# Smaller weight units, four buffers instead of two, and a page table loaded earlier

## The chip, the cores and the metric

The kernel runs on one core of a Trainium2 chip. The metric is the device time of one execution in microseconds (us). A core has a matrix engine (TensorE, PE in the rows, with its weight loads as PEld), a vector engine (VectorE, DVE), a scalar engine (ScalarE, ACT), a general engine (GpSimd, POOL), and a sync engine (SyncE, SP) that here only issues DMAs. Sixteen DMA engines move data between the main memory and the on-chip buffer.

## The reference, cut to what matters

A prompt of 256 tokens and eight samples of one token each go through two layers that share one set of weights; they are handled as one matrix of NT = 264 columns and 1024 features.

```
layer 0: x += 0.5*SwiGLU(rms(x)); x += W_out[gated delta net | differential attention](W_in rms(x)); x += 0.5*SwiGLU(rms(x))
layer 1: x += 0.5*SwiGLU(rms(x)); x += latent attention(rms(x));                                     x += 0.5*SwiGLU(rms(x))
y = rms(x)
swiglu(h) = (silu(h @ w_gate) * (h @ w_up)) @ w_down        # w_gate, w_up: 1024 x 2816, w_down: 2816 x 1024
past keys and values of a sample = pool[page_table[sample]]  # 16 pages of 128 rows
```

So there are four feed-forward parts (FFN 0 to 3), one mixer between 0 and 1 and one between 2 and 3. The samples attend to 2048 past rows each, which lie in pages that the page table names.

## The kernel before, in words

**Weights.** The host lays all weight matrices out as 2600 blocks of 128 x 128 float32 numbers in the order of their use. The class `Stream` (object `W`) brings them in units of 16 blocks (1 MB, 128 rows of 8 KB) into two buffers of the pool tag `raw` (`N_RAW = 2`, line 33). A piece is 4 blocks. `split` (line 618) turns a piece into a high part, written by ScalarE, and a low part, written by VectorE, in one of six places `whl`; three matrix products per block then give float32 accuracy. Splitting runs up to `LOOK = 5` pieces ahead of the blocks that PE uses. When the last piece of a unit is split, `used` (line 613) makes the next load into that buffer, by a DMA on the SP queue. A few weights of the second mixer are used whole, without a split (`whole`, line 650). `W.limit` holds the splitting back in each mixer, because its attention borrows the `whl` places, and `W.resume` lets it go on.

**Stages.** The first FFN is fed by `boot` (line 1082), which scales x by the norm weights and takes its squares. An FFN (line 864) computes 22 pairs of gate and up columns and then 8 down columns, block after block. The mixer of layer 0 (line 1143) interleaves the input projection `proj`, the prompt's and the samples' differential attention and the delta net. The mixer of layer 1 (line 1781) does the same for latent attention, and ends in `tail` (line 2057), the output projection.

**Past rows.** Two `Loader` objects gather strips of pages by indirect DMAs that GpSimd issues. `LK` gathers keys (tiles `dk`, 512 KB each, 64 of them, and later `mk`), `LV` gathers values (`dv`, 1 MB each, 32 of them, and later `mv`). They need the row numbers in `pt` and `ptk`, which `early` (line 1095) computes on VectorE from the page table. The first gathers are made in FFN 0: after column m, `side[m]()` hands a free place to a loader.

**The order of work.** The program is written as threads (generators). The class `Clock` (line 188) replays them with a cost estimate for every instruction and puts each instruction into its engine's queue in the order of the estimated starts, once, while the program is built; on the chip every queue runs in that fixed order. A DMA is estimated at 450 ns of the hardware queue, 700 ns of delay, its bytes at 360 GB/s on one pipe that all DMAs share, and 1000 ns (lines 460 to 467). Where the estimate leaves PE a gap, `keep_warm` (line 436) puts products of a constant into it that nobody reads (line 666). A thread can wait for a name (`yield from wait(...)`) that another thread makes available with `done.add`; a `flow` thread otherwise goes on as soon as few of its products are left to put into the queue.

**The start.** SP issues, in this order: the norm vectors, x in three parts with the first unit in three parts between and behind them, the second unit, the identity matrix, the page table, the constants, and the rest (lines 703 to 731).

Of the kernel before, what the change touches and what calls it, by code (L numbers as in the profile page):

```python
# [32 lines left out]
N_RAW = 2  # L33
# [87 lines left out]
N_UNITS = (N_BLOCKS + 15) // 16  # L121
# [21 lines left out]
class Virtual:  # L143
    """A tile whose place is chosen when its first instruction is put into a queue."""
# [5 lines left out]
class Slots:  # L150
    """Places of one shape for virtual tiles. The place of a tile is free again when its thread has gone past the
    segment that made it (keep: when the thread has called free) and its last instruction is in a queue."""
# [35 lines left out]
class Clock:  # L188
    """Puts the instructions that the threads create into the engine queues in the order of their
    estimated starts, so that no queue waits long at its head."""  # L190
# [16 lines left out]
    # -- tiles  # L207
# [48 lines left out]
    def when(self, r, write, eng=None):  # L256
        """When an instruction of `eng` may use the region."""
        n, p0, p1, lo, hi = r
        l = self.reg.get(n)
        if l is None and n[0] == "v" and n[1:].isdigit() and self.virtual[int(n[1:])].at is None:  # L260
            return self.virtual[int(n[1:])].slots.first(eng)[0]
        if l is None and self.prev.get(n):
            l, (p0, p1, lo, hi), write = self.reg.get(self.prev[n], ()), (0, 128, 0, 1 << 30), True
        t = 0.0
        for a in l or ():
            if a[0] < p1 and p0 < a[1] and a[2] < hi and lo < a[3]:
                if a[4]:
                    t = max(t, a[4] + self.lag(a[6], eng))
                if write and a[5]:
                    t = max(t, a[5] + self.lag(a[7], eng))  # L270
        return t
# [18 lines left out]
    # -- cost estimates  # L290
# [47 lines left out]
    # -- instructions  # L338
# [91 lines left out]
    def pe(self, t, c, cols, share):  # L430
        """The tensor engine's clock is halved in each tick after one in which few columns left the array."""
        if self.columns.get(int(t // self.TICK) - 1, 0.0) < self.FULL:
            c *= 2.0
        k = int((t + c) // self.TICK)
        self.columns[k] = self.columns.get(k, 0.0) + cols * share
        return t + c

    def keep_warm(self, t):
        """Matmuls that nobody reads, up to time t."""
# [52 lines left out]
    def add(self, name):  # L492
        """What the current thread has created so far makes `name` available."""
        if not self.cur:
            self.done[name] = 0.0
        else:
            self.cur.marks.append((name, self.seq))
            self.settle(self.cur)

    # -- threads: generators that yield None (go on when all that they issued is done), a time, or the  # L500
    # names they wait for
# [53 lines left out]
def hybrid_trunk_kernel(ctx: ExitStack, tc: tile.TileContext, wall, xT, wba, vecs, cst0, cst1, ident_d, convst,  # L555
# [29 lines left out]
    def service(thread, f, *a):  # L585
        """f's instructions in a thread of their own, which nobody waits for as a whole."""
# [5 lines left out]
    # ------------------------------------------------------------ weight stream  # L592
    class Stream:
        """The weights, 128 x 128 blocks in the order of their use; units of 16 blocks are loaded, pieces of 4 split into
        a high and a low part, except those that raw() hands out whole."""
# [7 lines left out]
        def dma(self, *parts):  # L603
            if self.u < N_UNITS:
                if self.u not in self.raw:
                    self.raw[self.u] = wp.tile([128, 2048], F32, tag="raw", name="raw", bufs=N_RAW)
                    self.left[self.u] = 16 // PIECE
                for a, b in parts or ((0, 2048),):
                    Q.dma_start(self.raw[self.u][:, a:b], wall[self.u][:, a:b])
                if not parts or parts[-1][1] == 2048:  # L610
                    self.u += 1
# [6 lines left out]
        def split(self):  # L618
# [4 lines left out]
            u, o = divmod(p * PIECE, 16)  # L623
# [11 lines left out]
        def advance(self, p):  # L635
            while self.p <= p + LOOK and self.p < self.limit and self.p * PIECE // 16 < self.u:
                self.split()
# [12 lines left out]
        def whole(self, use):  # L650
            """use(the next block); with float32 products for these there is nothing to split."""
            p, s = divmod(self.i, PIECE)
            u, o = divmod(self.i, 16)
# [11 lines left out]
    # in the tensor engine's gaps it multiplies a constant, so that its clock stays up  # L665
# [17 lines left out]
    def rsqrt(src, w, np_=128):  # L683
        """1/sqrt of a small tile on the vector engine."""
# [17 lines left out]
    # ------------------------------------------------------------ constants  # L702
# [8 lines left out]
    W.dma((1024, 2048))  # L711
    for _ in range(N_RAW - 1):
        W.dma()
# [10 lines left out]
    Q.dma_start(pt, ptab)  # L724
    cst = sb.tile([128, NCST], F32, tag="cst", name="cst0")
# [7 lines left out]
    # ------------------------------------------------------------ norm statistics  # L733
# [19 lines left out]
    def norm_rows(n, squares, scale, eps):  # L753
        """squares: n tiles [128, NT]. For tile i, rows 32 i and 32 i + 1 of the result add up to
        1 / sqrt(scale * (sum over the partitions) + eps)."""
# [32 lines left out]
    class Rstd:  # L788
        """The thread that computes mul / sqrt(scale * sum of acc over the partitions + eps), for every row; get()
        yields it to a thread that needs it."""  # L790
# [31 lines left out]
    # ------------------------------------------------------------ driver  # L822
# [7 lines left out]
    def flow(gen, bonus=0.0):  # L830
        """A thread that goes on as soon as its matrix products are in the queue."""
        return gen, True, bonus

    def urgent(gen, bonus=BONUS):
        """A thread whose instructions go first even if others could start a little earlier."""
# [8 lines left out]
    def lead(xh, xl, tags):  # L844
        """The first blocks of a projection; the last rows of x come latest, so the first two blocks alternate."""
# [17 lines left out]
    # ------------------------------------------------------------ FFN  # L863
    def ffn(f, wname, woff, rs, last=False, side={}):
        xh, xl = state["xw"]
        with tc.tile_pool(name=f"ffn{f}", bufs=1) as ap_:
# [21 lines left out]
            for m in range(MF):  # L888
# [14 lines left out]
                if m in side:  # L903
                    side[m]()
# [17 lines left out]
    # ------------------------------------------------------------ final norm  # L922
# [18 lines left out]
    def finish_y():  # L941
        """The statistics with the tokens on the partitions; a product with their diagonal spreads them."""
# [21 lines left out]
    # ------------------------------------------------------------ KV gather  # L964
# [5 lines left out]
    class Loader:  # L970
        """Gathers tiles of 32-row strips of four pages each, in order, into whichever slots are free."""
# [40 lines left out]
        def retire(self, tags):  # L1012
            """These slots are not filled again."""
# [8 lines left out]
    # ------------------------------------------------------------ one sample's softmax over its past  # L1022
    def scores(b, w, load, parts, SM, ready, cc, P, pT):
        """w [128, sub, 32]: the queries, one diagonal block for each page of a strip; parts: for each part
        of the features, its four strips' tiles. Leaves exponentials (strip, page, query row; key) in P,
        transposed in pT; returns the inverses of their sums."""
# [30 lines left out]
    def weigh(o, pT, load, strips, vs, dv):  # L1057
        """o [32 j + query row, dv]: the values weighed by pT."""
# [13 lines left out]
    # ============================================================ start  # L1072
# [22 lines left out]
    def early():  # L1095
        V.tensor_scalar(pt, pt, 32.0, vc("pi"), op0=OP.mult, op1=OP.add)
        for i in range(2):
            V.tensor_scalar(ptk[:, i, :], pt[:, 0:4 * NS], 2.0, float(i), op0=OP.mult, op1=OP.add)
        yield
# [42 lines left out]
    # ============================================================ layer 0 mixer  # L1142
    def mixer0():
        with tc.tile_pool(name="m0", bufs=1) as mp_:
# [16 lines left out]
            # ---- input projection  # L1161
# [70 lines left out]
            # ---- normalisation of four head blocks by their partition sums  # L1232
# [13 lines left out]
            # ---- gated delta net  # L1246
# [19 lines left out]
            def gdn():  # L1266
# [59 lines left out]
                # decay in (key, query) layout, 64-token chunks stacked two high  # L1326
# [12 lines left out]
                # Gram products  # L1339
# [60 lines left out]
                # token-major keys and values  # L1400
# [24 lines left out]
                # scan over the chunks  # L1425
# [29 lines left out]
            # ---- gated delta net, one step of each sample: four samples at a time, row 32 j + 4 i + h  # L1455
            # belongs to sample 4 t + j and head h (i: high, low and again high part of the update's operands)
# [110 lines left out]
            # ---- differential attention, prompt  # L1567
# [90 lines left out]
            # ---- differential attention, samples  # L1658
# [46 lines left out]
            # ---- output projection, one half of the rows at a time  # L1705
# [24 lines left out]
            def post_d():  # L1730
# [10 lines left out]
                # the samples: rows (head, sample), columns the head's features  # L1741
# [38 lines left out]
    # ============================================================ layer 1 mixer  # L1780
    def mixer1():
        with tc.tile_pool(name="m1", bufs=1) as mp_:
# [139 lines left out]
            # ---- prompt  # L1922
# [44 lines left out]
            # ---- samples  # L1967
# [43 lines left out]
            def mla_self():  # L2011
                yield from wait("ql0", "ql1", "qp", "ck")
                # scores of the new tokens with themselves: rows h, columns b
# [71 lines left out]
# ---- host side: layouts only  # L2085
def _blocks(w):
    """[K, M] -> [M/128, K/128, 128, 128] (m block, k block, row, column)."""
# [4 lines left out]
def _pack(inp):  # L2092
# [4 lines left out]
    def pairs(a):  # L2097
        """Blocks of two columns at a time, their first halves first."""
# [35 lines left out]
    if n % 16:  # L2134
        a = np.concatenate([a, np.zeros((16 - n % 16, 128, 128), f)], 0)
    return np.ascontiguousarray(a.reshape(N_UNITS, 16, 128, 128).transpose(0, 2, 1, 3)).reshape(N_UNITS, 128, 2048)

# [76 lines left out]
```

## Time and profile before

| | us |
|---|---|
| median of 3 runs | 1344.3 |
| range of the runs | 1342.52 to 1350.92 |
| span of the profiled execution, first to last instruction | 1297.2 |

The profiled execution's own device time is not listed apart from its span. The median of the runs lies 47.1 us above the span, which is time before the first and after the last instruction.

In the profile, busy time is given by engine, and idle time by what ended it. Rows of a view by windows give, for each stretch, the busy time of each engine with its count of instructions, the granted TensorE clock as a share of full speed (1.00 is 2.4 GHz, half of it is 1.2 GHz), the share of the 16 DMA engines' time that packets took, and the rate in GB/s. The chain of waits is followed back from the last instruction. Nearly all instructions go through one helper (line 457), so rows are told apart by the tiles that they write and read.

### The profile page before, as it was taken

The numbers are of one execution on the slowest core, as the hardware profiler recorded it, in microseconds if no ns is written. First come the engines' busy times: TensorE is split into PE (matmuls) and PEld (weight loads), VectorE is DVE, ScalarE is ACT, GpSimd is POOL, SyncE is SP. The second block draws the span as 40 slices with busy tenths as digits, with TensorE's granted clock in tenths as the row PEclk, the third lists the DMA queues.
The fourth block names the chain that finished last, engine by engine and source line by source line (L and its number), as shares of the span: only waits on it lengthen the run. The fifth ranks groups of instructions, "written<-read, shape, count | busy, mean of one in ns | idle before, by whom it ended". The sixth has DMA issues, their size and how long they took to land.

```text
span 1297.2 us, 28444 instructions
## 1 busy us (share of the span) xinstructions
PE 1274.9 (98%) x11569; PEld 1146.7 (88%) x11569; DVE 874.0 (67%) x1855; ACT 580.7 (45%) x1185; POOL 433.4 (33%) x526
## 2 busy tenths in 40 slices
PE   9999999999999999999999999999999999999997
PEld 7999999967676567999999999999876679999996
DVE  6777667687762767877766777766874449777652
ACT  5555544345411024555554555544432235555541
POOL 3643222355552412553422222212334523322221
PEclk9999999999996879999999999999999999999999
DMA  7776556898897563676755454555467955555551
GB/s 286 264 272 233 192 168 229 285 342 320 304 344 288 167 229 133 230 282 221 260 167 192 163 194 168 191 171 187 161 240 278 393 166 176 191 181 178 195 167 63
DMA packets 52163, 287.72 MB, mean 222 GB/s; under 512 B 6192, under 2 KB 6768, under 8 KB 27200
## 3 DMA queue, kind: packets, MB, share of 16 engines
q1 hardware_dynamic: 28912, 180.77, 40.0%
q0 software_dynamic: 23120, 105.13, 22.3%
q8 instruction: 91, 1.49, 0.4%
q14 instruction: 40, 0.33, 0.1%
HBM read 280.95 MB, written 5.03 MB: 220 GB/s over the span
## 4 chain that ended last, share of the span: by engine, by line
PE 86%; DVE 5%; DMA 3%; issue 2%; ACT 1%; POOL 1%; SPq 0%; POOLq 0%; ACTq 0%; DVEq 0%
PE ps_pd L457 40%; PE ps_pa L457 37%; PE ps_pc L457 5%; PE ps_po L457 3%; DVE whl L457 2%; PE ps_pe L666 2%; DMA dv<-in_vpool_dram,pt 2%; DMA raw<-in_wall_dram 1%; ACT whl L457 0%; DVE wxl L457 0%; DMA x<-in_xT_dram 0%; DVE QW L457 0%; DVE x L457 0%; POOL t L457 0%; DVE QR L457 0%
## 5 line engine op out<-in xcount | busy, mean ns | idle before, releaser
L457 DVE TENSOR_TENSOR whl<-raw,whl 128x512 fp32r<-128x512 f32 x642 | 486.0, 766 | 214.7 <-ACT whl L457 208.3
L457 ACT ACTIVATE whl<-raw 128x512 fp32r<-128x512 f32 x642 | 399.8, 630 | 371.9 <-PE ps_pa L457 195.9
L457 PE MATMUL ps_pa<-wxh,whl 128*128 128x264 f32 x1616 | 325.0, 286 | 1.8 <-ACT t L457 0.8
L457 PEld LDWEIGHTS ps_pa<-wxh,whl 128*128 128x128 f32 x1616 | 260.8, 188 | 11.0 <-issue 6.6
L457 PE MATMUL ps_pd<-wxh,whl 128*128 128x264 f32 x1152 | 233.9, 285 | 0.0
L457 PE MATMUL ps_pa<-wxl,whl 128*128 128x264 f32 x808 | 231.1, 286 | 0.0
L457 PEld LDWEIGHTS ps_pd<-wxh,whl 128*128 128x128 f32 x1152 | 187.6, 188 | 0.9 <-DVE whl L457 0.4
L457 POOL TENSOR_TENSOR t<-t,t 128x264 f32<-128x264 f32 (+1 forms) x100 | 83.1, 831 | 275.6 <-DVE t L457 275.4
L457 PE MATMUL ps_pd<-wxl,whl 128*128 128x264 f32 x576 | 164.1, 285 | 0.0
L457 PEld LDWEIGHTS ps_pa<-wxl,whl 128*128 128x128 f32 x808 | 151.8, 188 | 4.9 <-issue 4.5
L457 PE MATMUL ps_pd<-ah,whl 128*128 128x264 f32 x704 | 130.9, 284 | 0.0
L457 PE MATMUL ps_pa<-ah,whl 128*128 128x264 f32 x704 | 130.7, 284 | 0.0
L457 PEld LDWEIGHTS ps_pd<-ah,whl 128*128 128x128 f32 x704 | 110.0, 188 | 0.0
L457 PEld LDWEIGHTS ps_pa<-ah,whl 128*128 128x128 f32 x704 | 109.9, 188 | 0.0
L457 PEld LDWEIGHTS ps_pd<-wxl,whl 128*128 128x128 f32 x576 | 108.2, 188 | 0.8 <-issue 0.8
L457 PE MATMUL ps_pd<-al,whl 128*128 128x264 f32 x352 | 99.9, 284 | 0.0
L457 PE MATMUL ps_pa<-al,whl 128*128 128x264 f32 x352 | 99.7, 283 | 0.0
L457 POOL TENSOR_TENSOR al<-t,ah 128x264 fp32r<-128x264 f32 x88 | 76.9, 874 | 58.0 <-ACT ah L457 57.9
L457 POOL TENSOR_TENSOR t<-x 128x264 f32<-128x264 f32 x45 | 32.8, 730 | 189.0 <-DVE x L457 183.3
L457 POOL DMA_INDIRECT dk<-in_kpool_dram,ptk x57 | 58.8, 1031 | 56.9 <-PE ps_pc L457 45.2
L457 PE MATMUL ps_pd<-wya,whl 128*128 128x264 f32 x352 | 71.2, 284 | 0.0
L457 PE MATMUL ps_pa<-wya,whl 128*128 128x264 f32 x352 | 71.0, 284 | 0.0
(414 smaller groups left out, 1964.6 us busy)
## 6 DMA issues: line engine op xcount, KB each, us to landing
raw<-in_wall_dram SPq DMA_DIRECT2D x162, 1024.0 KB, 4.9
out_y_dram<-wya SPq DMA_DIRECT2D x4, 264.0 KB, 2.6
xh<-in_rec_dram SPq DMA_DIRECT2D x4, 256.0 KB, 9.5
xl<-in_rec_dram SPq DMA_DIRECT2D x4, 256.0 KB, 17.6
out_recs_dram<-xh SPq DMA_DIRECT2D x4, 256.0 KB, 7.1
out_recs_dram<-xl SPq DMA_DIRECT2D x4, 256.0 KB, 4.3
dk<-in_kpool_dram,ptk POOLq DMA_INDIRECT x57, 6.3
cst<-in_cst_dram SPq DMA_DIRECT2D x1, 838.5 KB, 8.7
```

Source lines behind the costliest of these rows:

```text
L457: f(*a, **k)
L666: clk.spare = lambda: nc.tensor.matmul(pe[0:32, 0:256], busy[:, 0:32], busy, start=True, stop=True)
```

## The change

- A unit has 8 blocks (512 KB, 128 rows of 4 KB), and there are four buffers. The bytes on chip are the same; 325 units take the place of 163. Every 16 in the stream's arithmetic becomes `UNIT`.
- At the start, the first unit comes in two parts, the second unit behind the last part of x, then the identity matrix and the page table, and the third and fourth unit behind the table.
- `early` makes the name "ptk" available once the row numbers are computed, and an FFN waits for that name before each hand-over of a place to a loader.
- Comments are taken out, which changes nothing.

```diff
-N_RAW = 2
+UNIT = 8
+N_RAW = 4
...
-N_UNITS = (N_BLOCKS + 15) // 16
+N_UNITS = (N_BLOCKS + UNIT - 1) // UNIT
...
                 if self.u not in self.raw:
-                    self.raw[self.u] = wp.tile([128, 2048], F32, tag="raw", name="raw", bufs=N_RAW)
-                    self.left[self.u] = 16 // PIECE
-                for a, b in parts or ((0, 2048),):
+                    self.raw[self.u] = wp.tile([128, UNIT * 128], F32, tag="raw", name="raw", bufs=N_RAW)
+                    self.left[self.u] = UNIT // PIECE
+                for a, b in parts or ((0, UNIT * 128),):
                     Q.dma_start(self.raw[self.u][:, a:b], wall[self.u][:, a:b])
-                if not parts or parts[-1][1] == 2048:
+                if not parts or parts[-1][1] == UNIT * 128:
                     self.u += 1
...
     Q.dma_start(x[:, 2:4, :], xT[:, 2:4, :])
     W.dma((512, 1024))
     Q.dma_start(x[:, 4:8, :], xT[:, 4:8, :])
-    W.dma((1024, 2048))
-    for _ in range(N_RAW - 1):
-        W.dma()
+    W.dma()
     ident = sb.tile([128, 128], F32, name="ident")
     Q.dma_start(ident, ident_d)
...
     Q.dma_start(pt, ptab)
+    for _ in range(N_RAW - 2):
+        W.dma()
     cst = sb.tile([128, NCST], F32, tag="cst", name="cst0")
...
                 if m in side:
+                    yield from wait("ptk")
                     side[m]()
...
             V.tensor_scalar(ptk[:, i, :], pt[:, 0:4 * NS], 2.0, float(i), op0=OP.mult, op1=OP.add)
+        done.add("ptk")
         yield
```

The host packs the blocks in units of `UNIT` accordingly.

## Rows read from the trace of the kernel before

**Rows 1.** The page: span, and busy time with its share and instructions.
```profile
span 1297.2 us, 28444 instructions
PE 1274.9 (98%) x11569; PEld 1146.7 (88%) x11569; DVE 874.0 (67%) x1855; ACT 580.7 (45%) x1185; POOL 433.4 (33%) x526
```

**Rows 2.** The page, chain of waits, shares of the span by line.
```profile
PE ps_pd L457 40%; PE ps_pa L457 37%; PE ps_pc L457 5%; PE ps_po L457 3%; DVE whl L457 2%; PE ps_pe L666 2%; DMA dv<-in_vpool_dram,pt 2%; DMA raw<-in_wall_dram 1%; ACT whl L457 0%; DVE wxl L457 0%; DMA x<-in_xT_dram 0%; DVE QW L457 0%; DVE x L457 0%; POOL t L457 0%; DVE QR L457 0%
```

**Rows 3.** Windows of 20 us: layer 1's output projection, and FFN 3.
```profile
1060.00:1080.00 20.00, 20.00 (x163) 19.54 (x162) 16.75 (x26) 11.94 (x23) 8.34 (x9) 1.00 0.61 205
...
1100.00:1120.00 20.00, 20.00 (x167) 20.00 (x167) 15.10 (x26) 11.44 (x23) 7.73 (x10) 1.00 0.52 165
```

**Rows 4.** Chain in order of time, FFN 0: start, us, what.
```profile
58.24 1.47 PE ps_pd L457 x12
```

**Rows 5.** Waits, whole span: engine, waited for, us in total, times, longest.
```profile
ACT whl L457 <- DMA raw<-in_wall_dram: 27.3, 22, 3.6
```

**Rows 6.** Tile raw: durations in ns min/median/max of its DMA issues; landing times.
```profile
L457 SPq DMA_DIRECT2D raw<-in_wall_dram x165: 327/328/655, 1.7 to 1263.4; - x165
...
DMA to landing us min/median/max: 3.6/4.9/9.7
```

**Rows 7.** DMA issues: count, KB each, median us from issue to landing.
```profile
raw<-in_wall_dram SPq DMA_DIRECT2D x162, 1024.0 KB, 4.9
...
dk<-in_kpool_dram,ptk POOLq DMA_INDIRECT x57, 6.3
...
raw<-in_wall_dram SPq DMA_DIRECT2D x2, 256.0 KB, 4.5
...
dv<-in_vpool_dram,pt POOLq DMA_INDIRECT x32, 9.5
...
pt<-in_ptab_dram SPq DMA_DIRECT2D x1, 32.0 KB, 7.5
```

**Rows 8.** DMA queues: packets, MB, share of 16 engines' span.
```profile
q1 hardware_dynamic: 28912, 180.77, 40.0%
q0 software_dynamic: 23120, 105.13, 22.3%
```

**Rows 9.** Timeline of GpSimd in layer 0's mixer: start, us, gather issue, idle before.
```profile
277.63 0.99 POOL L457 DMA_INDIRECT dk<-in_kpool_dram,ptk  x1 [0.30 <-issue]
```

**Rows 10.** Timelines at the mixer's start, ScalarE and PE: start, us, idle before.
```profile
219.28 1.68 ACT L457 ACTIVATE whl<-raw 128x512 fp32r<-128x512 f32 x3 [2.13 <-DMA raw<-in_wall_dram]
...
225.08 0.30 PE L457 MATMUL ps_pc<-ya,QW 128*32 128x128 f32 x2 [0.92 <-DVE QW L457]
```

**Rows 11.** Chain in order of time, layer 0's mixer: start, us, what.
```profile
354.48 11.93 DMA dv<-in_vpool_dram,pt
...
381.87 9.30 DMA dv<-in_vpool_dram,pt
```

**Rows 12.** Windows of 20 us in layer 0's mixer.
```profile
380.00:400.00 20.00, 18.91 (x275) 12.85 (x267) 12.20 (x34) 1.48 (x5) 9.83 (x11) 1.00 1.02 406
400.00:420.00 20.00, 20.00 (x122) 12.46 (x122) 0.00 (x0) 2.51 (x6) 4.29 (x5) 0.52 0.65 245
420.00:440.00 20.00, 20.00 (x138) 11.45 (x134) 15.46 (x38) 1.16 (x4) 6.48 (x6) 0.88 0.35 115
440.00:460.00 20.00, 19.71 (x148) 11.13 (x148) 11.93 (x22) 0.97 (x3) 6.96 (x7) 0.71 0.74 253
460.00:480.00 20.00, 20.00 (x194) 12.86 (x193) 11.10 (x45) 6.72 (x18) 4.21 (x5) 0.77 0.45 143
```

**Rows 13.** Windows, the constant's products alone (line 666): sum over the span.
```profile
sum 1300.00, PE 47.13 PEld 29.01; mean PE 0.73 PEld 0.45
```

**Rows 14.** Timelines of SP and VectorE at the start: the table and x.
```profile
5.92 0.74 SPq L457 DMA_DIRECT2D pt<-in_ptab_dram  x1
...
12.68 0.49 DVE L457 SCALAR_TENSOR_TENSOR wxl<-x,vec,wxh 128x264 fp32r<-128x264 f32 x1
...
20.49 0.20 DVE L457 TENSOR_SCALAR pt<-pt,vec 128x64 int32<-128x64 int32 x1
```

More of the change, by code (lines that the diff above doesn't have):

```diff
@@ L622, in split @@
                 return
-            u, o = divmod(p * PIECE, 16)
+            u, o = divmod(p * PIECE, UNIT)
             r = self.raw[u][:, o * 128:o * 128 + w]
@@ L635, in advance @@
         def advance(self, p):
-            while self.p <= p + LOOK and self.p < self.limit and self.p * PIECE // 16 < self.u:
+            while self.p <= p + LOOK and self.p < self.limit and self.p * PIECE // UNIT < self.u:
                 self.split()
@@ L652, in whole @@
             p, s = divmod(self.i, PIECE)
-            u, o = divmod(self.i, 16)
+            u, o = divmod(self.i, UNIT)
             self.i += 1
@@ L2133, in _pack @@
     assert n == N_BLOCKS, (n, N_BLOCKS)
-    if n % 16:
-        a = np.concatenate([a, np.zeros((16 - n % 16, 128, 128), f)], 0)
-    return np.ascontiguousarray(a.reshape(N_UNITS, 16, 128, 128).transpose(0, 2, 1, 3)).reshape(N_UNITS, 128, 2048)
+    if n % UNIT:
+        a = np.concatenate([a, np.zeros((UNIT - n % UNIT, 128, 128), f)], 0)
+    return np.ascontiguousarray(a.reshape(N_UNITS, UNIT, 128, 128).transpose(0, 2, 1, 3)).reshape(N_UNITS, 128, UNIT * 128)
 def _layout(inp):
```

## The prediction

> **What bounds the kernel now.** I read the page first, then the chain of waits, then PE's stretches of 20 us, and last the rows of the weight tiles. PE is busy for 1274.9 of 1297.2 us [rows 1], and the chain runs through PE's products for most of the span; waits for weight loads hold 1% of it and waits for gathered values 2% [rows 2]. So a faster weight stream is worth something only where PE stands, or does work that nobody reads, because weights are late.
>
> In the feed-forward parts it never does: FFN 3 shows PE at 20.00 of 20 us, full clock, DMA engines half idle [rows 3]. A piece of 4 blocks is 12 products in 1.47 us [rows 4], so a block takes 0.367 us, a unit of 16 blocks 5.9 us, a unit of 8 blocks 2.9 us. PE's lost time is elsewhere: 1297.2 - 1274.9 = 22.3 us idle [rows 1], 47.1 us in products of the constant [rows 13], and the dips of the clock in layer 0's mixer, (1 - 0.52 + 1 - 0.88 + 1 - 0.71 + 1 - 0.77) x 20 = 22.4 us [rows 12]. That pool of some 92 us is all that this change could draw on, and most of it lies in attention and the delta net, where the gathers and small products set the pace.
>
> The sum is made against the profiled execution's span of 1297.2 us. The runs shown have a median of 1344.3, 47.1 us more, which the change does not touch, so a difference in the span goes over to the median as it is.
>
> **The change part by part.**
>
> *Cover of a load.* Before, a unit's load is requested when the last piece of its predecessor in that buffer has been split; one whole unit, 16 blocks or 5.9 us of PE's work, is then ahead. A load lands after 4.9 us in the median, 9.7 at worst [rows 6]. That is tight, and it shows: ScalarE waited for a weight load 22 times, 27.3 us together, 3.6 at most [rows 5]. After, three units, 24 blocks or 8.8 us, are ahead. The trace has no load of 512 KB by itself on SP; the nearest rows are 4.5 us for 256 KB, taken at the crowded start, and 4.9 for 1 MB [rows 7], so I take 4.7. The margin grows from 1.0 to 4.1 us, and nearly all of the 27.3 us of ScalarE's waits should go. What that is worth on PE is another thing: splitting runs five pieces ahead, 5 x 1.47 = 7.4 us, twice the longest wait, and so in the feed-forward parts I cost it at nothing; the cover is that lead. If the lead were gone, each wait would count whole, 27.3 us.
>
> *Where the lead is gone.* At the head of layer 0's mixer, a wait of 2.13 us of ScalarE for weights stands in front of VectorE's work on the queries, and PE then stands 0.92 us [rows 10]. I take 0.9 off; between 0 and 2.1. In layer 1's output projection PE is busy throughout and holds 163 products against 167 in a plain stretch [rows 3]; 4 products of 0.12 us are 0.5 us. There the old unit border fell in the middle of the value weights of latent attention, 8 blocks early, and the new one does not. I take 0.8 for this and the hand-over behind it, between 0 and 2.
>
> *Gathers beside weights.* In layer 0's mixer the DMA engines are full, 1.02 of their time from 380 to 400 us [rows 12], and two waits for values are on the chain, 11.9 and 9.3 us [rows 11]. The bytes stay the same. A weight load in front of a gather is now half as large: 512 KB less at the 406 GB/s of that stretch is 1.3 us. Both waits together, were they cut to the median landing of 9.5 [rows 7], would give 2.4 us; I take 2.0. The ends are 0, as the other half of the weights comes just behind, and 2 x (11.9 + 9.3)/2 - 2 x 4.9 = 11.4, if such a gather landed as fast as a weight load.
>
> *Smaller rows and more DMAs.* The queue of the gathers has the smaller packets (105.13 MB in 23120, 4.5 KB each, against 6.3 KB on the weights' queue), and moves 105.13 MB / (0.223 x 1297.2 us) = 363 GB/s of full share against 180.77 / (0.400 x 1297.2) = 348 [rows 8]. Rows of 4 KB cost nothing by that. SP issues a load in 0.33 us [rows 6]; 162 more are 53 us of SP's time over the whole program, and one per 2.9 us is far from filling it. On SP's queue stand also the sample states and the outputs; the fixed order keeps them where their estimates put them, and they cost an issue each.
>
> *The table.* It was issued at 5.92 us and landed after 7.5, so at 13.4; VectorE first used it at 20.49 [rows 7, 14], 7 us later. After, 1 MB less is in front of it, and it can only come sooner. The first gather waits for the row numbers before and after, and keys gathered in FFN 0 are not used before the mixer, 200 us on: nothing. What can cost is that the plan now puts the table's three small operations among the splits of x, the last of which runs at 12.68 [rows 14]; if the table is later than estimated, VectorE stands in front of the first FFN. From 12.68 back to 13.4 is 0.7 us; I take 0, between 0 and 2. The wait for "ptk" holds the FFN's thread, not an engine: behind it stand the products of column 2 onward. By then two columns are queued (4 x 2 pieces of 1.47 us), and the name is there once three operations are in VectorE's queue; nothing.
>
> *The plan.* Every weight load has another estimate, so the order on all engines is made anew, in the mixers above all. It takes out or adds pieces of the 92 us without a sign that the rows would give. A tenth to a fifth of that pool, 9 to 18 us, is my estimate of the scatter.
>
> Sum: -0.9 - 0.8 - 2.0 = -3.7 us, 0.3%: 1344.3 - 3.7 = 1340.6, as a round figure **1340**. With the ends of the terms, 1344.3 - 2.1 - 2 - 11.4 = 1329 to 1344.3 + 2 = 1346.
>
> The Trainium skill, page "DMA: Bandwidth & Descriptors", section "Rules for kernel authors", asks for at least 1 MiB per DMA for full bandwidth, which speaks against this change; its section on the anatomy of one DMA fits 2.0 us plus bytes at 436 GB/s, for the GpSimd path. An estimate by that page: 3.2 us for 512 KiB. The rows above disagree with a loss here, since loads overlap.
>
> **The rivals.**
>
> *Hidden anyway.* The feed-forward parts, where the loads are, have no gap [rows 3], and the mixers' terms come out as nothing: 1344, within the noise. For it: the 1% of the chain [rows 2]. It is in the same band as the forecast.
>
> *Faster, by the mixer.* The half-clock stretch from 400 to 420 us follows a stretch in which PE waited for values (18.91 busy of 20, clock still 1.00) [rows 11, 12]. If smaller loads bring these values sooner and the stretch stays at full clock, 0.48 x 20 = 9.6 us go beside the forecast's 3.7: 1331. With the gathers' far end as well, 9.4 more: 1321. Against it: dips to 0.71 and 0.77 follow where few weights are loaded.
>
> *Slower, by the mixer.* The new plan uses up the projection's products, PE's only filler there, before the gathers have landed, as weights now stand 24 blocks ahead; more of the delta net then runs at the lower clock. One more 20 us of such a stretch costs 9.6 us [rows 12]. It decides from the second one on: 1340.6 + 19.2 = 1360. For it: the stretch from 400 to 420 has exactly this form. Against: the count of blocks before the mixer's limit is the same.
>
> *Slower, by the loads.* If one load at a time were on its way, 8 blocks would cost 4.7 us in place of 2.9, and 4 x 528 / 8 = 264 units of the feed-forward parts 1.8 x 264 = 475 us. By the page's 3.2 us it would be about 0.3 x 264 = 79 us, 1420. Against it: gathers of 512 KB are issued 1.3 us apart and land after 6.3 [rows 7, 9], so about five are on their way at once; two more loads in flight are nothing new.
>
> **How the numbers follow.** About 1%, 13.4 us, is what a measurement of this kernel can tell from no change. Forecast 0.41 and hidden anyway 0.20, both within 1%: 0.61; faster by the mixer 0.25; slower by the mixer 0.12; slower by the loads 0.02. The forecast's own range is 1331 to 1352, its terms' ends with the plan's scatter. For 8 in 10, I leave out the loads, most of the slower mixer and the far end of the faster one: 1320 to 1356.
>
> **What would show it.** In the profile after: waits of ScalarE for weight loads well under 27.3 us; a load's landing near 4.7 us, and not above 8.8; feed-forward stretches still at 167 products; PE's gap of 0.92 at the mixer's head gone; the waits for values on the chain near 9.5 us; the table's operations on VectorE before 13 us. The prediction is wrong if the feed-forward stretches lose products, or if idle time, the constant's products and the clock's dips change by more than 13 us together.

## The result, and the profile after

The kernel before has a median of 1346.38 us (1342.52 to 1350.92), the changed kernel 1362.56 us (1356.37 to 1365.95): a ratio of 1.0115, 95% interval 1.0083 to 1.0146. It is slower by 1.15%, outside the predicted range and on the side to which the prediction gave a chance of 0.14.

One point about the yardstick comes first, since all later numbers hang on it. The profiled execution of the changed kernel took 1359.81 us with a span of 1357.5, so 2.3 us lie outside the span, and not 47.1, as the sections above took it. The kernel before, run again on three chips, has medians of 1298.21, 1297.85 and 1301.53 us; one of its profiled executions took 1297.49 us with a span of 1295.6. So rows 1 to 14 fit a chip on which this kernel runs in 1298 to 1302 us, and the first timing fits another, some 3.6% slower. Ratios below are taken only between runs that shared a chip. Profiles are set side by side across the three faster chips, on which the kernel before differs by 0.3%. The ratio carries over: the changed kernel gave 1.0117 on one of them.

The page of the changed kernel, first profile (slower chip): span, busy time, the weights' and the gathers' queue (packets, MB, share of 16 engines' span), and the issues of weight loads.

```profile
span 1357.5 us, 29006 instructions
PE 1304.5 (96%) x11643; PEld 1163.5 (86%) x11643; DVE 873.1 (64%) x1855; ACT 584.1 (43%) x1185; POOL 421.4 (31%) x526
...
q1 hardware_dynamic: 52096, 180.26, 41.3%
q0 software_dynamic: 23120, 105.13, 21.4%
...
raw<-in_wall_dram SPq DMA_DIRECT2D x324, 512.0 KB
```

The waits of ScalarE for weight loads in the same profile, and a stretch of FFN 3 (columns as in [rows 3]).

```profile
ACT whl L458 <- DMA raw<-in_wall_dram: 1.9, 3, 1.2
```
```profile
1160.00:1180.00 20.00, 20.00 (x168) 20.00 (x167) 15.46 (x27) 11.44 (x23) 7.04 (x9) 1.00 0.56 170
```

The loads do what they were meant to do: 27.3 us of waits [rows 5] have become 1.9, and the feed-forward parts were and are full, 167 products in 20 us [rows 3], now 168. The time has gone elsewhere. To see where, the changed kernel is set beside the kernel before on equally fast chips. First its weight tile and the head of the mixer (as [rows 6, 10]), from the run f1 of the next section, then two stretches of layer 0's mixer (as [rows 12]).

```profile
DMA to landing us min/median/max: 3.0/3.6/12.1
```
```profile
224.35 0.30 PE L458 MATMUL ps_pc<-ya,QW 128*32 128x128 f32 x2 [0.84 <-DVE QW L458]
```
```profile
280.00:300.00 20.00, 18.56 (x154) 11.33 (x154) 13.84 (x53) 6.35 (x23) 8.75 (x12) 1.00 0.90 321
420.00:440.00 20.00, 20.00 (x93) 11.39 (x92) 5.06 (x20) 2.31 (x7) 1.88 (x2) 0.57 0.26 89
```

The same two stretches of the kernel before, run again:

```profile
280.00:300.00 20.00, 19.86 (x148) 13.42 (x145) 16.70 (x56) 8.66 (x25) 8.83 (x13) 1.00 0.93 354
...
420.00:440.00 20.00, 20.00 (x139) 11.19 (x139) 14.80 (x37) 1.16 (x4) 6.48 (x6) 0.91 0.43 140
```

A load lands after 3.6 us instead of 4.9, yet PE's gap at the head is still there (0.84 us, before 0.92), and layer 0's mixer has lost ground. The whole loss can be read off with the prediction's own pool: PE's idle time, the constant's products, and the clock's dips. Over 200 to 600 us, which holds this mixer in every run, the windows of PE and of line 666/667 end in these sums. Kernel before, run again: all of PE, then the constant's products.

```profile
sum 400.00, PE 394.55; mean PE 19.73
sum 400.00, PE 23.97; mean PE 1.20
```

Changed kernel:

```profile
sum 400.00, PE 389.72; mean PE 19.49
sum 400.00, PE 34.25; mean PE 1.71
```

Idle time is 400 less the first sum, 5.5 against 10.3 us; the constant takes 24.0 against 34.3; and the dips, (1 - clock) x 20 summed over the 20 windows, are 20.6 against 24.0. Together 50.0 against 68.5 us, 18.5 more, where the spans differ by 1311.8 - 1295.6 = 16.2. The loss lies in this mixer, and the pool has moved by more than the 13 us that the prediction named as its sign of being wrong.

### The profile page after: what moved, and what is told of

It reads as the page before. It is cut to its first block, busy times and chain, and to the rows that moved or that the text cites. A ratio compares the mean times of both kernels' runs of the same rounds, so it can differ in the third digit from the quotient of the medians.

```text
span 1357.5 us, 29006 instructions
## 1 busy us (share of the span) xinstructions
PE 1304.5 (96%) x11643; PEld 1163.5 (86%) x11643; DVE 873.1 (64%) x1855; ACT 584.1 (43%) x1185; POOL 421.4 (31%) x526
## 3 DMA queue, kind: packets, MB, share of 16 engines
q1 hardware_dynamic: 52096, 180.26, 41.3%
## 4 chain that ended last, share of the span: by engine, by line
PE 86%; DVE 5%; issue 4%; DMA 1%; another core or an unknown queue 1%; POOL 1%; ACT 1%; POOLq 0%; DVEq 0%; ACTq 0%
PE ps_pd L458 39%; PE ps_pa L458 37%; PE ps_pc L458 5%; PE ps_po L458 3%; PE ps_pe L667 2%; DVE whl L458 1%; DMA out_recs_dram<-xl 1%; DVE t L458 1%; DMA dv<-in_vpool_dram,pt 1%; DVE QR L458 0%; DVE QW L458 0%; DVE yb L458 0%; ACT whl L458 0%; DVE wxl L458 0%
## 5 line engine op out<-in xcount | busy, mean ns | idle before, releaser
L458 PE MATMUL ps_pa<-wxh,whl 128*128 128x264 f32 x1616 | 329.0, 288 | 4.8 <-DVE t L458 3.7
L458 PEld LDWEIGHTS ps_pa<-wxh,whl 128*128 128x128 f32 x1616 | 265.1, 191 | 14.0 <-issue 7.9
L458 POOL TENSOR_TENSOR t<-t,t 128x264 f32<-128x264 f32 (+1 forms) x100 | 79.9, 799 | 305.3 <-DVE t L458 300.9
L458 POOL TENSOR_TENSOR al<-t,ah 128x264 fp32r<-128x264 f32 x88 | 69.3, 788 | 46.7 <-ACT ah L458 46.6
```

The lines of the kernel that those rows point to most:

```text
L458: f(*a, **k)
```

## The experiments

The theory after the result: apart from the loads and the constant's products the program's instructions are the same, but the planner, given other transfers, put them into the queues in another order, and the order of layer 0's mixer is worse. The rival: the smaller loads themselves, by their rows of 4 KB or by colliding with the gathers. Each ratio below is to the kernel before on the same chip; the table at the end of this section gives the pool of each run.

**e0_before_again.** The kernel before, unchanged.

> The kernel before, unchanged, for a second profile beside the others. The first profile of it has a span of 1297.2 us, 45 to 54 us under its four timed runs (1342.5 to 1350.9), while the changed kernel's profiled run has a span of 1357.5 us and a time of 1359.8, only 2.3 us apart. Theory A (47 us of every run lie outside the span): this profile's span is near 1297 and its time near 1345. Theory B (the first profile caught an execution that was itself some 45 us shorter): span and time are some 2 us apart, the span near 1343, and the extra time is in the mixers, where the gathers are.

1297.49 us, span 1295.6. The offset of 47.1 us was not time outside the span.

**e1_new_loads_old_order.** The changed kernel's loads and start; the queues of PE, VectorE, ScalarE and GpSimd in the order of the kernel before, so without the wait for "ptk".

```diff
-        while True:
-            best = None
...
+        for code in self.plan:
...
+            i, e = divmod(code, 6)
...
+                    op = every[i].q[ENG[e]][0]
...
+                    self.emit(op)
```

`plan` is the recorded order: which thread's next instruction goes into which engine's queue.

> The changed kernel's loads (units of 8 blocks, four buffers, table ahead of the third unit) with the instruction order of the kernel before on PE, VectorE, ScalarE and GpSimd, instruction by instruction, the constant's products included. Theory 1 (the loss comes from the order that the plan made anew): as the kernel before, ratio 0.995 to 1.003, or 3.7 us faster, as my sum had it. Theory 2 (the loss comes from the smaller loads themselves): as the changed kernel, ratio 1.008 to 1.015.

Ratio 1.001 (0.9994 to 1.0026). Its waits, its landing, and its queue of weights:

```profile
ACT whl L502 <- DMA raw<-in_wall_dram: 1.0, 2, 0.8
```
```profile
DMA to landing us min/median/max: 3.3/3.6/8.6
```
```profile
q1 hardware_dynamic: 52096, 180.26, 41.7%
```

The loads alone cost nothing and bring nothing, although 24 us of ScalarE's waits are gone. The rival falls.

**e2_old_loads_new_order.** Units of 16 blocks in two places, with the page table ahead of the second unit; the order of the changed kernel from the start to FFN 2, that of the kernel before from there, replayed as in e1.

```diff
-UNIT = 8
-N_RAW = 4
+UNIT = 16
+N_RAW = 2
```

> The loads of the kernel before (units of 16 blocks, two buffers, the table ahead of the second unit) with the changed kernel's instruction order from the start to the third FFN, and the order before from the mixer of layer 1 on (the changed order of that mixer needs four buffers). Theory 1 (the order): ratio 1.008 to 1.015, all of the loss, as most of the order's differences are in layer 0's mixer. Theory 2 (the loads): ratio 0.997 to 1.003.

Ratio 1.0173 (1.0145 to 1.0200). The order alone does all of the harm, and perhaps more than in the changed kernel (1.0117 in f1, whose interval ends at 1.0159). The chain of waits holds a load here (start, us, what), and the waits of PE for queries (tile `QW`) and for values (`dv`) are longer than in f1 (columns as in [rows 5]); first e2, then f1:

```profile
239.82 8.03 DMA raw<-in_wall_dram
```
```profile
PE ps_pc L500 <- DVE QW L500: 5.9, 5, 2.9
PE ps_po L500 <- DMA dv<-in_vpool_dram,pt: 5.7, 2, 4.0
```
```profile
PE ps_pc L458 <- DVE QW L458: 2.3, 4, 0.8
...
PE ps_po L458 <- DMA dv<-in_vpool_dram,pt: 0.8, 1, 0.8
```

The 8.03 us are the load's own time on the chain, and PE multiplies through most of them. PE's own rows in e2, at the mixer's head and behind that load:

```profile
229.31 0.30 PE L500 MATMUL ps_pc<-ya,QW 128*32 128x128 f32 x2 [2.86 <-DVE QW L500]
...
249.97 1.95 PE L500 MATMUL ps_pc<-dk,QW 128*32 128x128 f32 x64 [1.07 <-DVE QW L500]
```

So an order made for weights that come early, given weights that come late, does make PE wait, 2.86 us at the head (0.84 in f1) and 1.07 behind that load. More of the surplus is in waits for values. All of PE's idle time from 200 to 600 us is 17.7 us in e2 and 10.3 in f1.

**e3_halves_old_order.** The kernel before and its order; each load of 1 MB made by two DMAs of 512 KB, with rows of 4 KB.

```diff
-                for a, b in parts or ((0, 2048),):
+                for a, b in parts or ((0, 1024), (1024, 2048)):
```

> The kernel before in its own order with two buffers of 16 blocks, but each unit is brought by two DMAs of 512 KB with rows of 4 KB. Theory 2 in the form that small rows or twice as many DMAs cost: ratio 1.004 to 1.015. Theory 1 (the order): ratio 0.997 to 1.003.

Ratio 1.0004 (0.9988 to 1.0021); a half lands after 4.5 us in the median, a whole one after 4.8 in e0. Rows of 4 KB and twice the DMAs cost nothing here.

**f1_after.** The changed kernel as it is, on one of the faster chips.

> The changed kernel as it is, on a chip where the kernel before runs beside it. Theory 'the order alone': the loss is that of the re-made order in layer 0's mixer, which cost 1.0173 with the old loads; so 1.014 to 1.021 here, and the same holes in PE as there (some 50 products of the constant between 280 and 300 us, the delta net's Gram products 25 to 40 us later than in the kernel before). Theory 'the loads give some back': the finer loads repay a part, 1.008 to 1.013. Theory 'both cost': over 1.022.

Ratio 1.0117 (1.0076 to 1.0159), inside the second of the three theories, that the finer loads give a little back in the order that was made for them; as this interval and that of e2 overlap, how much they give back is open. Now the hole itself, the stretch in which PE has little but the constant's products. PE of this run around the end of the key columns (start, us, what, count, and in brackets the idle time before it):

```profile
271.87 0.28 PE L458 MATMUL ps_pa<-wxl,whl 128*128 128x264 f32 x1
272.08 0.86 PE L458 MATMUL ps_pc<-dk,QW 128*32 128x128 f32 x24
...
275.68 2.17 PE L458 MATMUL ps_pc<-dk,QW 128*32 128x128 f32 x72
277.78 0.39 PE L458 MATMUL ps_pc<-SM,ident 128*128 128x8 f32 x2
278.46 0.39 PE L458 MATMUL ps_pa<-wxh,whl 128*128 128x264 f32 x1
...
281.78 1.91 PE L667 MATMUL ps_pe<-busy 128*32 128x256 bf16 x16
...
286.88 1.05 PE L667 MATMUL ps_pe<-busy 128*32 128x256 bf16 x8
...
290.33 1.81 PE L667 MATMUL ps_pe<-busy 128*32 128x256 bf16 x15
...
292.52 0.29 PE L458 MATMUL ps_pa<-wxh,bal 128*8 128x264 f32 x1 [0.38 <-DVE bal L458]
...
296.02 0.28 PE L458 MATMUL ps_pa<-wxh,whl 128*128 128x264 f32 x1
```

VectorE in the same run, and then in the kernel before:

```profile
287.07 0.17 DVE L458 TENSOR_SCALAR rsi<-t 128x9 int32<-128x9 int32 x1
...
291.89 0.47 DVE L458 STREAM_TRANSPOSE t<-ny 128x288 f32<-128x288 f32 x1
292.28 0.18 DVE L458 TENSOR_TENSOR bal<-wb,bah 128x64 fp32r<-128x64 f32 x1
293.39 1.45 DVE L458 SCALAR_TENSOR_TENSOR S<-S,ps_pd 128x264 f32<-128x264 f32 x4
```
```profile
278.39 0.22 DVE L457 TENSOR_TENSOR bal<-wb,bah 128x64 fp32r<-128x64 f32 x1
```

And PE in the kernel before:

```profile
270.72 0.28 PE L457 MATMUL ps_pa<-wxh,whl 128*128 128x264 f32 x1
...
272.83 0.64 PE L457 MATMUL ps_pc<-dk,QW 128*32 128x128 f32 x16
...
281.24 0.28 PE L457 MATMUL ps_pa<-wxh,bal 128*8 128x264 f32 x1
...
284.62 0.28 PE L457 MATMUL ps_pa<-wxh,whl 128*128 128x264 f32 x1
```

In the kernel before, the last key column has its last product at 270.7, and the 128 score products of one sample follow; meanwhile its tail is done, VectorE splits the small weight `wb` (tile `bal`) at 278.4, and the projection goes on with the products of `wb` and, from 284.6, the query columns. In the new order one last product of that column stands behind the same scores, at 278.5. Its tail is late by that, the key norm (tiles `rsi` to `ny`) takes VectorE first, and `bal` comes at 292.3, behind all of it. The projection is one thread: its query columns cannot pass the products of `wb`. So PE has nothing to fill with, is handed 52 products of the constant between 280 and 300, and begins the query columns 11.4 us later. The delta net's Gram products (tile `S` by `S`) start at 350.3 in the kernel before and at 363.5 here, its scan (tile `S` by `SS`) at 422.8 and 439.6.

**f2_split_early.** The changed kernel, with `wb` split in FFN 0.

```diff
     def early():
...
+        yield
+        hilo(bh, bl, wb)
         yield
...
                     if name == "gk3":
-                        bh = sb.tile([128, KD, 8], F32R, name="bah")
-                        bl = sb.tile([128, KD, 8], F32R, name="bal")
-                        hilo(bh, bl, wb)
```

> The changed kernel with one thing moved: the split of the small weight wb (one ScalarE and one VectorE operation) is made in FFN 0 instead of behind the fourth key column of layer 0's mixer; the order is made anew. Theory 'the projection stands behind bal': in the new order that VectorE operation stands behind the whole key norm (at 300.7 us, before at 278.4), PE is handed 49 products of the constant meanwhile, and the delta net starts 12 us later. With it out of the way PE has the next projection columns in that gap: ratio to the kernel before 1.003 to 1.011, under 25 products of the constant from 280 to 300. Rival 'the loss comes from the later holes': 1.015 to 1.020.

Ratio 1.0076 (1.0051 to 1.0101), no product of the constant between 280 and 300, Gram products at 352.0 and scan at 427.3, 11.5 and 12.3 us sooner than in f1. As the whole order was made again, this supports the hole as a cause rather than isolates it. But of the 11.5 us only 0.41%, 5.3 us, came out, and the intervals of f1 and f2 overlap. The rest was given back later:

```profile
400.00:420.00 20.00, 20.00 (x115) 13.34 (x115) 2.28 (x12) 3.39 (x10) 4.33 (x5) 0.51 0.65 241
420.00:440.00 20.00, 20.00 (x108) 11.11 (x106) 6.95 (x19) 1.34 (x5) 3.80 (x4) 0.55 0.16 58
```

PE stays near half its clock (granted 0.51 and 0.55, where 0.50 is 1.2 GHz) for two stretches instead of one; the dips are 34.4 us, in f1 24.0.

**f3_split_early_14.** As f2, with 14 products ahead of a flow thread.

```diff
-    AHEAD = 12
+    AHEAD = 14
```

> As the run before this, and a flow thread may have 14 products in its queue instead of 12 before it is asked for more, which makes the order anew once more. If the order alone decides, this is another draw from the same urn: anywhere from 0.995 to 1.02; an order with fewer than 160 products of the constant in layer 0's mixer (the kernel before has 154) should come out within 0.5% of the kernel before. This one has fewer, 124: 0.993 to 1.003. If the finer loads themselves cost, it stays above 1.01.

Ratio 1.0008 (0.9989 to 1.0028): with the changed kernel's loads and another order the loss is gone.

**f4_nudge350** and **g3_nudge370.** The kernel before; only the rate by which the planner estimates transfers is changed.

```diff
-                self.pipe = max(self.pipe, t + 700.0) + 4.0 * self.size(out) * out.shape[0] / 360.0
+                self.pipe = max(self.pipe, t + 700.0) + 4.0 * self.size(out) * out.shape[0] / 350.0
```

> The kernel before, with its own loads and its own start; only the number by which the plan estimates a transfer is changed, 350 GB/s instead of 360. Nothing that runs is different but the order. Theory 'any re-made order is a draw, and the one of before is a picked one': slower, 1.005 to 1.02. Rival 'only the new loads lead the plan astray': 0.998 to 1.003.

> The kernel before with the plan's transfer rate at 370 GB/s instead of 360, all else as it was. The order changes again, but holds nearly as few products of the constant in layer 0's mixer as before (158 against 154; at 350 GB/s it was 189). Theory 'a draw, and its worth is in the holes': 0.998 to 1.004. Rival 'every departure from the order before costs': 1.006 to 1.012.

1.008 (1.0054 to 1.0105) at 350, and 0.9966 (0.9944 to 0.9988) at 370, a little better than expected and the only kernel here whose interval lies below 1. Nothing that runs differs but the order, with the constant's products that it holds.

**g4_old_loads_split_early.** The kernel before with f2's edit.

> The kernel before, its loads and all numbers of the plan; only the split of wb is made in FFN 0, which takes two operations out of layer 0's mixer and can hold nothing up by itself. Theory 'a draw': the order that comes out has 195 products of the constant in that mixer instead of 154, so slower, 1.003 to 1.012. Rival 'less work in the mixer is less time': 0.995 to 1.000.

1.0036 (1.0014 to 1.0057): two operations less in the mixer, and slower.

**h2_new_mixer1.** The changed kernel's loads, the old order up to FFN 2, the changed kernel's own from layer 1's mixer on, by the same replay (the edit is that of e1, with another recorded order).

> The changed kernel's loads; up to the end of FFN 2 the order of the kernel before, from the mixer of layer 1 on the changed kernel's own order. Theory 'layer 0's mixer alone': 0.998 to 1.003, as with the old order throughout (1.001). Rival 'the re-made order of layer 1's mixer costs too': over 1.004, towards the changed kernel's 1.0117.

0.9981 (0.9961 to 1.0002). Layer 1's mixer has no part in the loss.

**g2_draw.** f3 with other weights of the threads in layer 0's mixer.

```diff
-BONUS = 150.0
+BONUS = 180.0
...
-    TOL = 60.0
+    TOL = 62.0
...
-            run(urgent(rs.thread()), urgent(post_d(), 40.0), diff_p(), diff_s(), diff_v(), urgent(gdn_s(), 80.0), urgent(gdn(), 80.0), dpv(), flow(proj(), 0.0), post_g())
+            run(urgent(rs.thread()), urgent(post_d(), 60.0), diff_p(), diff_s(), diff_v(), urgent(gdn_s(), 120.0), urgent(gdn(), 85.0), dpv(), flow(proj(), 0.0), post_g())
```

> The changed kernel with the early split of wb, 14 products ahead, and other weights for the threads of layer 0's mixer; the order that leaves fewest products of the constant in that mixer (122) among some 290 orders made. If loads and order were all, and better than the kernel before was to be had by a draw: 0.993 to 0.998. If the order before is already near the floor of what orders give: 0.998 to 1.003.

0.9991 (0.9969 to 1.0012): no better than the kernel before.

The pool of each run, 200 to 600 us of its profile, in us; "products" is how many products of the constant the order holds in layer 0's mixer.

| kernel | products | idle | constant | dips | sum | span | ratio |
|---|---|---|---|---|---|---|---|
| before (e0) | 154 | 5.5 | 24.0 | 20.6 | 50.0 | 1295.6 | 1 |
| e1, e3, h2 (old order there) | 154 | 9.4, 6.0, 6.4 | 23.1, 23.7, 23.7 | 17.2, 18.8, 18.8 | 49.7, 48.5, 49.0 | 1297.5, 1294.3, 1295.0 | 1.001, 1.0004, 0.9981 |
| e2 | 235 | 17.7 | 34.5 | 27.6 | 79.8 | 1324.7 | 1.0173 |
| f1 (the change) | 235 | 10.3 | 34.3 | 24.0 | 68.5 | 1311.8 | 1.0117 |
| f2 | 174 | 8.1 | 25.6 | 34.4 | 68.2 | 1308.7 | 1.0076 |
| f4 | 189 | 7.5 | 28.1 | 27.4 | 63.0 | 1306.6 | 1.008 |
| g4 | 195 | 11.5 | 30.1 | 15.4 | 57.0 | 1300.0 | 1.0036 |
| g3 | 158 | 12.6 | 24.1 | 19.2 | 56.0 | 1297.5 | 0.9966 |
| f3 | 124 | 14.1 | 18.4 | 22.4 | 54.9 | 1299.4 | 1.0008 |
| g2 | 122 | 11.4 | 19.4 | 22.2 | 53.0 | 1295.5 | 0.9991 |

Measured from e0, the sum follows the span in the other eleven to within 5.1 us. Each span is that of one execution, and the chips differ, so differences of that size say nothing: g3 has 6.0 us more of the pool than e0 and a ratio below 1. The count of products alone does not decide: f2 has fewer than g4 and is slower, by its dips.

## Why the prediction was wrong

**The plan** is the step that failed. The prediction saw that the order would be made anew and put the scatter of that at 9 to 18 us; f1's 18.5 us of the pool are just above it. But it took the scatter "without a sign that the rows would give", put it into the sum at nothing, gave the slow side 0.14, and made its ranges narrower than its own terms: 1346, the high end of the other terms, and 18 are 1364, which would have held the result, and the ranges end at 1352 and 1356. What the runs showed in its place: the same loads in the old order take 1.001 of the time (e1), the new order alone costs 1.0173 (e2), and the loss is in layer 0's mixer (the pool; h2 frees layer 1's).

Whether the rows had a sign is argued and not shown. An order in which PE is busy for 98% of the span [rows 1], with a pool of 92 us in 1297, should leave more to lose than to win. On the chip, the new orders that were not chosen for few of the constant's products (f1, f2, g4, and f4, chosen for many) are slower, at ratios of 1.0117, 1.0076, 1.0036 and 1.008. Of those known to hold few, g3 is faster by 0.34%, f3 is level, and so is g2, which holds the fewest among some 290 orders. So the best of them won 0.34% where the change lost 1.17%; how new orders fall on average is not shown. In hindsight, a centre some 5 us above the time before, the mean of f2, f4, g3 and g4 (1.004), with a high end near +20, would have held the result.

**Cover of a load.** Right in what it says of the loads: the waits of 27.3 us nearly went (1.9; 5.3 in f1, 1.0 in e1), and in the feed-forward parts that is worth nothing. The landing was mis-sized, 3.6 us and not 4.7. The Trainium skill, page "DMA: Bandwidth & Descriptors", section "Anatomy of one DMA — SWDGE (gpsimd) path", has bytes at 436 GB/s, for DMAs that GpSimd issues; by that, 512 KiB less are an estimated 1.2 us less. Between 4.8 in e0 and 3.6 in e1, that is what SP's loads show too.

**Where the lead is gone.** -0.9 and -0.8 us were wrong. e1 has the new loads and the old order. ScalarE no longer waits for weights there, and PE's gap is still 0.93 us:

```profile
225.17 0.30 PE L502 MATMUL ps_pc<-ya,QW 128*32 128x128 f32 x2 [0.93 <-DVE QW L502]
```

So VectorE's own work on the queries ended that wait, not the load in front of it. Layer 1's mixer gave nothing clear (h2, 0.9981 to 1.0002).

**Gathers beside weights.** -2.0 us did not come, and could not: the 11.9 and 9.3 us that the term was read from are the gathers' own times on the chain, not waits of PE. What PE waited for values in that trace, over the whole span, is 1.4 us:

```profile
PE ps_po L457 <- DMA dv<-in_vpool_dram,pt: 1.4, 2, 1.1
```

So the 2.0 were too much, and the far end of 11.4 us had nothing behind it. In e1 a gather of values lands after 8.1 us in the median, in e0 after 9.2, as foreseen. The chain holds two of them in e0 (9.36 and 8.80 us) and one in e1 (12.26), and PE waits 0.5 and 0.6 us for values: the ratio is 1.001.

**Smaller rows and more DMAs.** Wrong in the rate, right in the cost. The weights' bytes took 180.77 MB / (0.398 x 1295.6) = 351 GB/s of full share in e0 and 180.26 / (0.417 x 1297.5) = 333 in e1, 5% more engine time per byte. It costs no time (e1, e3). The Trainium skill, page "DMA: Bandwidth & Descriptors", section "Rules for kernel authors", asks for at least 1 MiB per DMA for the most bandwidth. The 5% agree in direction; no run here shows a loss of time by it.

**The table.** Right in the cost, which is nothing: the first of its three operations runs on VectorE at 11.48 us in the changed kernel, before at 20.49, between splits of x of which the last now runs at 12.84 (before 12.68). The other two run at 13.25 and 20.57, where the prediction had all three before 13. The wait for "ptk" moves no instruction: the order made without it is the same on every engine.

**The offset of 47.1 us** was not time outside the span; it lay between the profiled execution and the timed ones, as far as the runs tell a difference between chips. The ratio survived it, and it did not spoil the forecast.

**The rivals.** "Slower, by the mixer" had the place, and by luck the size (1360 against 1362.56), but not the mechanism. It had the projection run out of products because weights came 24 blocks ahead. e2 has no such lead and the same hole (49 of the constant's products from 280 to 300 us, `bal` at 300.7), and products were not lacking: they stood behind `bal` in their own thread. That rival's 19.2 us were all lower clock; the clock's dips made 3.4 of the 18.5 us. "Slower, by the loads" is refuted by e1. "Hidden anyway" is what the loads alone do. What is not shown is why the planner, told of smaller loads, moved just that one product behind the scores; f4 and g4 show only that other small edits make other orders too, and these two were worse.

## What to carry to other kernels

Where a planner writes the order of the queues from estimates, every edit draws a new order: freeze the old one to measure the edit, and judge the draw by itself. Where the scatter of the draw is as large as the change, carry it whole into the range of the forecast, and where the order before leaves little idle, give the slow side more of it: the orders measured here ran from 0.9966 to 1.0173. A transfer on the chain of waits counts with all of its own time; what the critical engine waited for it is in the rows of waits, and it can be far less (1.07 of 8.03 us in e2). Waits of an engine that runs ahead of the critical one are no gain in reserve: 24 us of them went for a ratio of 1.001.

## What the runs showed of the hardware

The same kernel takes 1298 to 1302 us on three chips and took 1346 us in the first timing, some 3.6% more, while the ratio of two kernels moved from 1.0115 to 1.0117. That the first timing was on a fourth chip is inferred. And filling a hole need not shrink the pool: f2 has 8.6 us less of the constant's products than f1 and 10.4 us more of dips, most of them over 100 us further on, and its sum stays at 68.2 against 68.5.
